# A line of 64 bytes between the weight ring and the blocks of a two-layer decoder

## The chip, the cores and the metric

The kernel runs on one core of one Trainium2 chip. The time is device microseconds of one execution, the median of several runs; lower is better. TensorE (PE in the profile, with its weight loads apart as PEld) multiplies, VectorE (DVE) and ScalarE (ACT) do elementwise work, GpSimd (POOL) fills constants, and SyncE (SP) issues most of the loads from memory.

## The reference, cut to what matters

Two layers over 256 tokens of width 2048 in fp32. Each layer has a mixer and a feed-forward part, each with a norm before it, a shift and a scale made from a vector c, a norm behind it, a gate made from c, and a residual add.

```python
for i in range(DEPTH):
    mixer, aw, ab, m_pre, m_post, f_pre, f_post, wg, wu, wd = layers[i]
    sh_m, sc_m, gt_m, sh_f, sc_f, gt_f = ada_modulation(c, aw, ab)   # silu(c) @ w + b, in 6 parts
    h = rmsnorm(x, m_pre) * (1.0 + sc_m) + sh_m
    x = x + gt_m * rmsnorm(mixer(h), m_post)
    h = rmsnorm(x, f_pre) * (1.0 + sc_f) + sh_f
    x = x + gt_f * rmsnorm(swiglu(h, wg, wu, wd), f_post)
```

The first mixer runs a diagonal state space (S5) and a gated delta rule beside each other, the second a gated linear attention; their projections and the feed-forward matrices (2048 x 5632 and back) are most of the work. The output is x, 256 x 2048.

## The kernel before

All weights stream through a ring of tiles. A tile `w` of 128 x 1024 fp32 (4,096 bytes in each partition) is loaded on SP's queue; ScalarE casts it to `wh` (line 159) and VectorE makes the remainder `wl` = w - wh (line 160). The activations are split the same way beforehand, into hi and lo halves (`hhi`/`hlo`, `ahi`/`alo` and so on). Three matmuls then give one fp32-like product: hi x hi, hi x lo, lo x hi (lines 234 to 236 in `mm3`). Of the two operands of a matmul, one (`lhsT`) is loaded into the array as weights, 128 x 128 at a time, and the other (`rhs`) streams through it.

Three routines use `mm3`. `gemm_wide` and `gemm_feat` load 128 columns of a weight tile into the array and stream 256 tokens of the activations: 256 columns a matmul. `gemm_tok` loads 128 tokens of the activations and streams 512 columns of the weight tile: 512 columns a matmul. `gemm_wide` does the gate and up projections of the feed-forward parts, `gemm_feat` the mixers' inputs (one call of it is only 16 columns wide), `gemm_tok` the rest. At the end of some products, the last weights are "held": they are cast into tiles of the block pool instead of the ring (`hwh`, `hwl`), and the matmuls of the second half of the tokens come after all those of the first half.

The order of the work is a list-scheduled program order with priorities; side streams (the shift, scale and gate vectors from `ada_w`, the S5 and delta rule parts) are advanced at fixed rates by `tick`. Nothing of this is touched by the change.

What is touched is where tiles lie in SBUF, the on-chip memory of 128 partitions. Each pool takes one stretch of bytes in every partition, one behind the other:

| pool | what it holds | first byte before | after | first byte modulo 1,024, before and after |
|---|---|---|---|---|
| cst | masks, ones, small vectors | 16,512 | 16,512 | 128, 128 |
| ring | 6 `w`, 3 `wh`, 3 `wl` of 4,096 bytes | 22,912 | 22,912 | 384, 384 |
| sm | small tiles of many sizes, the accumulator `acc` first | 72,064 | 72,064 (the new line), `acc` at 72,128 | 384, 448 (`acc`) |
| blk | 32 blocks of 4,096 bytes: x, hhi, hlo, ahi, alo, hwh, hwl, ... | 97,600 | 97,664 | 320, 384 |

Ring tiles and blocks are multiples of 4,096 bytes long, so all of a pool lie at the same place modulo 1,024. A slice of 128 columns is 512 bytes long, one of 256 columns 1,024 bytes. The operands of a ring-fed matmul thus lie 64 bytes apart (modulo 512) before.

Of the kernel before, what the change touches and what calls it, by code (L numbers as in the profile page):

```python
# [12 lines left out]
F32 = mybir.dt.float32  # L13
# [9 lines left out]
P = 128  # L23
# [4 lines left out]
LINE = 16  # L28
# [15 lines left out]
class Net:  # L44
# [49 lines left out]
    def consts(s):  # L94
        nc = s.nc

        def mask(name, op, cm, step, base=0):
            t = s.cst.tile([P, P], F32, name=name)
            nc.gpsimd.memset(t, 1.0)
            nc.gpsimd.affine_select(out=t, in_=t, pattern=[[step, P]], compare_op=op, fill=0.0, base=base, channel_multiplier=cm)  # L100
            return t

        s.ident = mask("ident", ALU.is_equal, 1, -1)
        s.uinc = mask("uinc", ALU.is_ge, -1, 1)
        s.ustr = mask("ustr", ALU.is_gt, -1, 1)
        s.lstr = mask("lstr", ALU.is_gt, 1, -1)
        s.ones = s.cst.tile([P, P], F32, name="ones")
        nc.gpsimd.memset(s.ones, 1.0)

        s.sel = s.cst.tile([P, LINE], F32, name="sel")[:, 0:1]  # L110
        nc.vector.tensor_reduce(out=s.sel, in_=s.ident[:, 0::32], axis=AX.X, op=ALU.add)
# [1502 lines left out]
```

## Time and profile before

| | us |
|---|---|
| median of 3 runs | 2570.17 |
| lowest, highest | 2564.59, 2575.0 |
| the profiled execution | 2571.89 |
| its span | 2570.1 |
| its TensorE busy | 2471.8 |
| its VectorE, ScalarE, GpSimd busy | 1731.2, 1110.6, 85.8 |
| mean granted TensorE clock | 0.981 |

The span is the time from the first to the last instruction of the profiled execution; about 2 us of the time lie around it. The first 640 us are the shift and scale of the first norm, the first mixer and its output; up to about 1400 the first feed-forward part runs, up to about 1850 the second mixer, and then the second feed-forward part. Busy times of matmuls overlap, because one starts before the one ahead has ended, so the page's mean of one matmul is longer than the distance between two starts.

### The profile page before, as it was taken

The page shows a single profiled execution, that of the slowest core. Times are in us where ns is not written, and L with a number is a line of the kernel's source. Part 1 is how long each engine was busy: PE and PEld are TensorE (multiplying, and loading weights), DVE is VectorE, ACT ScalarE, POOL GpSimd, SP SyncE. Part 2 cuts the span into 40 slices and gives each one's busy share as a digit, 9 for nine tenths or more (in the row PEclk, how much of TensorE's full clock was granted, in tenths as well). Part 3 has the DMA queues.
Part 4 walks back from the last instruction along what each step waited for, and adds up shares of the span by engine and source line. Part 5 has one row for each costly group of instructions (what it writes and reads, how often), then busy time and mean ns, then how long its engine had stood idle before and what let it go on. Part 6 is the DMA issues. An engine that isn't in the chain of part 4 may idle for free.

```text
span 2570.1 us, 41866 instructions
## 1 busy us (share of the span) xinstructions
PE 2471.8 (96%) x16822; PEld 2181.0 (85%) x16822; DVE 1731.2 (67%) x2274; ACT 1110.6 (43%) x1396; POOL 85.8 (3%) x135
## 2 busy tenths in 40 slices
PE   5999999987999999999999999999999999999998
PEld 2577989976899899988987898788799889988996
DVE  6766787689677767777778676677655444555456
ACT  3354543445434444333435633444544444443443
POOL 1120001000000000000000000000000000000000
PEclk8999999998999999999999999999999999999999
DMA  8887557577788889898886596788467666666664
GB/s 280 303 249 238 176 189 269 178 268 240 240 291 295 308 287 313 293 310 315 289 275 216 160 301 210 251 282 276 168 210 220 191 196 191 196 192 194 193 193 140
DMA packets 299012, 615.62 MB, mean 240 GB/s; under 512 B 24368, under 2 KB 61680, under 8 KB 298816
## 3 DMA queue, kind: packets, MB, share of 16 engines
q1 hardware_dynamic: 294240, 604.32, 71.4%
q0 software_dynamic: 2304, 4.93, 0.6%
q10 hardware_dynamic: 2272, 3.68, 0.4%
q8 instruction: 132, 2.16, 0.3%
q14 instruction: 64, 0.52, 0.1%
HBM read 610.10 MB, written 2.10 MB: 238 GB/s over the span
## 4 chain that ended last, share of the span: by engine, by line
PE 82%; DVE 7%; DMA 6%; ACT 3%; issue 2%; POOL 0%; ACTq 0%; DVEq 0%; SPq 0%
PE mm L236 24%; PE mm L235 24%; PE mm L234 24%; DMA w<-in_ada_w_dram 5%; PE tp L329 2%; DVE wl L160 2%; DVE small L355 1%; PE tp L365 1%; ACT small L421 1%; ACT small L462 1%; PE tp L1296 1%; PE tp L1290 1%; PE tp L1049 1%; PE tp L400 0%; DMA w<-in_w_out_dram 0%
## 5 line engine op out<-in xcount | busy, mean ns | idle before, releaser
L159 ACT CAST wh<-w 128x1024 fp32r<-128x1024 f32 x722 | 758.2, 1051 | 1100.3 <-PE mm L235 549.4
L160 DVE TENSOR_TENSOR wl<-w,wh 128x1024 fp32r<-128x1024 f32 x722 | 876.5, 1221 | 480.9 <-ACT wh L159 479.3
L236 PE MATMUL mm<-hhi,wl 128*128 128x256 f32 (+1 forms) x3104 | 866.9, 279 | 14.3 <-DVE wl L160 14.3
L234 PE MATMUL mm<-hhi,wh 128*128 128x256 f32 (+1 forms) x3104 | 867.6, 280 | 0.0
L235 PE MATMUL mm<-hlo,wh 128*128 128x256 f32 (+1 forms) x3104 | 864.9, 279 | 0.0
L236 PEld LDWEIGHTS mm<-hhi,wl 128*128 128x128 f32 (+1 forms) x3104 | 582.5, 188 | 19.0 <-DVE wl L160 17.2
L234 PEld LDWEIGHTS mm<-hhi,wh 128*128 128x128 f32 (+1 forms) x3104 | 583.3, 188 | 4.1 <-issue 1.2
L235 PEld LDWEIGHTS mm<-hlo,wh 128*128 128x128 f32 (+1 forms) x3104 | 584.0, 188 | 2.1 <-issue 1.0
L355 DVE SCALAR_TENSOR_TENSOR small<-w,silu_c,small 128x1024 f32<-128x1024 f32 x288 | 370.6, 1287 | 185.8 <-DMA w<-in_ada_w_dram 176.8
L236 PE MATMUL mm<-wh,alo 128*128 128x512 f32 x656 | 258.3, 394 | 0.0
L235 PE MATMUL mm<-wl,ahi 128*128 128x512 f32 x656 | 256.9, 392 | 0.0
L234 PE MATMUL mm<-wh,ahi 128*128 128x512 f32 x656 | 256.7, 391 | 0.0
L234 PE MATMUL mm<-wh,hhi 128*128 128x512 f32 x440 | 177.4, 407 | 6.8 <-DVE hhi L467 3.7
L235 PE MATMUL mm<-wl,hhi 128*128 128x512 f32 x440 | 177.0, 403 | 3.8 <-DVE wl L160 3.8
L236 PE MATMUL mm<-wh,hlo 128*128 128x512 f32 x440 | 175.6, 400 | 0.2 <-DVE hlo L468 0.2
L235 PEld LDWEIGHTS mm<-wl,ahi 128*128 128x128 f32 x656 | 123.2, 188 | 29.2 <-DVE wl L160 0.6
L234 PEld LDWEIGHTS mm<-wh,ahi 128*128 128x128 f32 x656 | 123.2, 188 | 27.0 <-ACT wh L159 0.5
L236 PEld LDWEIGHTS mm<-wh,alo 128*128 128x128 f32 x656 | 123.3, 188 | 25.6
L234 PEld LDWEIGHTS mm<-wh,hhi 128*128 128x128 f32 x440 | 83.8, 192 | 25.5 <-DVE hhi L467 4.4
L235 PEld LDWEIGHTS mm<-wl,hhi 128*128 128x128 f32 x440 | 84.6, 192 | 23.9 <-DVE wl L160 5.4
L236 PEld LDWEIGHTS mm<-wh,hlo 128*128 128x128 f32 x440 | 84.6, 192 | 20.1 <-DVE hlo L468 0.8
L329 PE MATMUL tp<-w,silu_c 128*32 128x512 f32 x384 | 68.9, 640 | 10.1 <-ACT silu_c L323 5.4
(432 smaller groups left out, 2433.2 us busy)
## 6 DMA issues: line engine op xcount, KB each, us to landing
w<-in_ada_w_dram SPq DMA_DIRECT2D x384, 512.0 KB, 5.2
w<-in_ffn_gate_dram SPq DMA_DIRECT2D x176, 512.0 KB, 4.5
w<-in_ffn_up_dram SPq DMA_DIRECT2D x176, 512.0 KB, 4.5
w<-in_ffn_down_dram SPq DMA_DIRECT2D x176, 512.0 KB, 4.5
w<-in_w_in_dram SPq DMA_DIRECT2D x160, 512.0 KB, 5.0
w<-in_w_out_dram SPq DMA_DIRECT2D x64, 512.0 KB, 5.4
w<-in_s_glu_w_dram SPq DMA_DIRECT2D x8, 512.0 KB, 4.8
x<-in_x_dram SPq DMA_DIRECT2D x4, 512.0 KB, 6.5
```

Of the source, the lines that this page charges most:

```text
L159: s.nc.scalar.copy(hi, x)
L160: s.subs.append(s.nc.vector.tensor_tensor(out=lo, in0=x, in1=hi, op=ALU.subtract).ins)
L234: mm(ps, lhsT=lhs[0], rhs=rhs[0], start=st, stop=False)
L235: mm(ps, lhsT=lhs[0], rhs=rhs[1], start=False, stop=False)
L236: mm(ps, lhsT=lhs[1], rhs=rhs[0], start=False, stop=en)
L329: s.nc.tensor.matmul(ps[32 * j : 32 * j + 32, :], lhsT=lhsT, rhs=w, start=first, stop=last)
L355: nc.vector.scalar_tensor_tensor(out=acc, in0=wv[:, 0], scalar=s.sc[:, g : g + 1], in1=acc, op0=ALU.mult, op1=ALU.add)
L365: s.nc.tensor.matmul(ps[:, m : m + 1], lhsT=acc[:, m * P : m * P + P], rhs=e[:, 0:1], start=True, stop=True)
L421: s.nc.scalar.activation(out=dump[:, : int(x.free_size())], in_=x, func=AF.Square, accum_out=out)
L462: nc.scalar.activation(out=hf[:, js], in_=ps[:, js], func=AF.Identity, scale=S[:, k : k + 1], bias=H[:, k : k + 1])
L1049: nc.tensor.matmul(pp[:, i * 64 : i * 64 + 64], lhsT=s.s5_win[ig][e][:, i * P : i * P + P], rhs=us[:, i * 64 : i * 64 + 64], start=True, s ...
L1290: nc.tensor.matmul(pp[:, n * 64 : n * 64 + 64], lhsT=LT[m][:, n * P : n * P + P], rhs=Tv[:, n, :, 0, :], start=True, stop=True)
```

## The change

A tile `line` of 16 floats (64 bytes in a partition) is taken from the small pool before anything else of that pool, and set to zero; nothing reads it. All small tiles and all blocks lie 64 bytes further on; the constants and the ring stay. Ring and blocks then both lie at 384 modulo 1,024.

```diff
         s.ustr = mask("ustr", ALU.is_gt, -1, 1)
         s.lstr = mask("lstr", ALU.is_gt, 1, -1)
+
+        s.line = s.sm.tile([P, LINE], F32, tag="line", name="line", bufs=1)
+        nc.gpsimd.memset(s.line, 0.0)
         s.ones = s.cst.tile([P, P], F32, name="ones")
         nc.gpsimd.memset(s.ones, 1.0)
```

On POOL, at the start of the program, the masks and constants are filled in this order before:

```order
L100 AFFINE_SELECT lstr<-lstr 128x128
L108 MEMSET ones 128x128
L1135 MEMSET lev 128x256
L1140 AFFINE_SELECT lev<-lev 128x64 x3
L1141 AFFINE_SELECT lev<-lev 128x64 x3
```

And on POOL at the same place after (all lines behind the change are numbered three higher):

```order
L100 AFFINE_SELECT lstr<-lstr 128x128
L109 MEMSET line 128x16
L111 MEMSET ones 128x128
L1138 MEMSET lev 128x256
L1143 AFFINE_SELECT lev<-lev 128x64 x3
```

The new memset stands between the mask `lstr` and `ones`. On every engine all other instructions stand in the same order as before, the 13,920 matmuls of lines 234 to 236 (237 to 239 after) included.

## The prediction

> **What bounds the kernel now.** I read the page first (busy time, chain), then the busy time by stage, then the groups of matmuls, and then the starts of single matmuls, since the change touches nothing but addresses.
>
> ```profile
> span 2570.1 us, 41866 instructions
> PE 2471.8 (96%) x16822; PEld 2181.0 (85%) x16822; DVE 1731.2 (67%) x2274; ACT 1110.6 (43%) x1396; POOL 85.8 (3%) x135
> PE 82%; DVE 7%; DMA 6%; ACT 3%; issue 2%; POOL 0%; ACTq 0%; DVEq 0%; SPq 0%
> ```
>
> TensorE is busy for 96% of the span and is 82% of the chain that ended last. A change of a few nanoseconds per matmul therefore reaches the end, unless something else is waiting just behind. By stage (columns: PE, PEld, DVE, ACT, POOL busy, granted clock, DMA share, GB/s):
>
> ```profile
> 256.00:640.00 384.00, 358.38 (x2585) 312.11 (x2584) 301.80 (x487) 177.22 (x272) 20.66 (x25) 0.94 0.66 220
> 640.00:1440.00 800.00, 780.00 (x5350) 715.54 (x5349) 583.86 (x586) 335.80 (x391) 15.83 (x23) 0.99 0.84 285
> 1440.00:1850.00 410.00, 401.20 (x2198) 340.34 (x2196) 300.55 (x433) 195.09 (x260) 8.38 (x12) 0.99 0.73 237
> 1850.00:2570.00 720.00, 710.10 (x5019) 660.85 (x5017) 370.46 (x349) 297.76 (x310) 0.35 (x1) 1.00 0.61 192
> ```
>
> From 1850 on nothing but TensorE can be the bound: DMA is 61% busy and DVE half. From 640 to 1440 DMA is 84% busy, so some of a gain there may be lost. The first 640 us hold most of the idle time and half their waits are of other engines.
>
> **The matmuls that the change concerns.** In each, one operand comes from the ring (wh, wl) and the other from a block (hhi, ahi, ...). The name before the comma streams through the array, the one after it is the weight that was loaded.
>
> ```profile
> L234 PE MATMUL mm<-hhi,wh 128*128 128x256 f32 x3072 | 858.6, 280 | 0.0
> L234 PE MATMUL mm<-wh,ahi 128*128 128x512 f32 x656 | 256.7, 391 | 0.0
> L234 PE MATMUL mm<-wh,hhi 128*128 128x512 f32 x440 | 177.4, 407 | 6.8 <-DVE hhi L467 3.7
> L234 PE MATMUL mm<-wh,yhi 128*128 128x512 f32 x104 | 41.3, 397 | 0.0
> L234 PE MATMUL mm<-wh,yahi 128*128 128x512 f32 x64 | 26.6, 416 | 1.2 <-ACT y L490 1.2
> L234 PE MATMUL mm<-wh,ybhi 128*128 128x512 f32 x48 | 19.9, 425 | 3.8 <-ACT wh L159 3.8
> ```
>
> Each row stands for three (lines 234, 235, 236), so there are 9,216 with 256 columns, and 3 x 1,312 = 3,936 with 512 columns. The durations overlap; what counts is the distance from one start to the next.
>
> **Step 1: 512 columns.** The trace holds the state after the change already. Held weights (hwh, hwl) are blocks themselves, so there both operands lie at the same place within 1,024 bytes. The ring's lie 64 bytes apart. First and last of 189 ring matmuls, then of 47 held ones:
>
> ```profile
> 2279.79 0.39 PE L234 MATMUL mm<-wh,ahi 128*128 128x512 f32 x1
> ...
> 2322.82 0.39 PE L236 MATMUL mm<-wh,alo 128*128 128x512 f32 x1
> ...
> 1384.40 0.39 PE L235 MATMUL mm<-hwl,ahi 128*128 128x512 f32 x1
> ...
> 1394.82 0.39 PE L236 MATMUL mm<-hwh,alo 128*128 128x512 f32 x1
> ```
>
> Ring: 43.03 / 188 = 0.2289 us. Held: 10.42 / 46 = 0.2265 us. The other held stretches settle at the same 0.2267, and the ring's long ones all at 0.2289. The difference is 2.2 ns, and 2.2 ns x 3,936 = 8.7 us. Summed pair by pair over the timeline, the ring's 512-column starts lie 9.5 us beyond 226.67 ns each. Some of that comes right after a wait, where held matmuls also need several to settle. I take 8 us of TensorE time as gone.
>
> **Step 2: 256 columns.** Here the timeline shows two rhythms in the same code, each kept for hundreds of matmuls. By weight loads in four stretches (columns: PEld busy and count, clock, DMA share, GB/s), three slow, the last fast:
>
> ```profile
> 1470.10:1543.20 73.10, 73.10 (x622) 1.00 0.87 280
> 1882.00:2011.50 129.50, 129.50 (x1102) 1.00 0.67 212
> 953.50:1026.60 73.10, 73.10 (x622) 1.00 0.87 297
> 2102.20:2275.60 173.40, 173.40 (x1532) 1.00 0.63 195
> ```
>
> A count includes one or two that reach in over the edge. Slow: 73.10 / 620.5 = 117.8 ns; fast: 173.4 / 1530.4 = 113.3 ns. The fast one is just half of the 226.67 ns of step 1, so I take it for the undisturbed rate. The clock is 1.00 in all four, and DMA is as busy in a slow one (0.67) as in the fast one (0.63), so neither sets the rhythm; it is chosen when a stretch starts and then stays. The three slow stretches cost 2,341 x 4.45 ns = 10.4 us. With the shorter ones and the starts after waits, the 256-column starts lie 16.0 us beyond 113.33 ns each, summed pair by pair.
>
> No 256-column pair of full width lies at distance 0 before. The nearest evidence is the 16-column projection of the second mixer, in which the weight moves on by 64 bytes with each slice of K while the block's place within 1,024 bytes stays. The matmuls of line 234, one per slice (two others between):
>
> ```profile
> 1438.04 0.28 PE L234 MATMUL mm<-hhi,wh 128*16 128x256 f32 x1
> ...
> 1438.38 0.28 PE L234 MATMUL mm<-hhi,wh 128*16 128x256 f32 x1
> ...
> 1438.74 0.28 PE L234 MATMUL mm<-hhi,wh 128*16 128x256 f32 x1
> ...
> 1439.08 0.28 PE L234 MATMUL mm<-hhi,wh 128*16 128x256 f32 x1
> ...
> 1439.42 0.28 PE L234 MATMUL mm<-hhi,wh 128*16 128x256 f32 x1
> ```
>
> Steps of 0.34, 0.36, 0.34, 0.34 us. At the first row the weight is 256 bytes on from the block (0 modulo 256); the slow step belongs to 64 and 128 bytes on. The same four-slice pattern comes back twice in this pass, and at a distance of 0 modulo 256 every matmul of it starts after 113 or 114 ns. So distance decides, with a period of 256 bytes here, and 0 is a good place. The weights are loaded 16 columns wide there, not 128, which is why this is not proof. Bounds for the 256-column matmuls: all at 113.3 gains 16.0 us; all at 117.8 instead of their mean of about 115.05 loses 2.75 ns x 9,216 = 25 us. I take the near end, less 2 us for restarts after waits (an estimate): 14 us.
>
> **Step 3: what else moves.** The small pool and the blocks move by 64 bytes together, so their distance to each other stays. Distances to the ring and the constants change for DVE and ACT too. The trace has both distances:
>
> ```profile
> L160 DVE TENSOR_TENSOR wl<-w,wh 128x1024 fp32r<-128x1024 f32 x720 | 875.7, 1224 | 480.9 <-ACT wh L159 479.3
> L160 DVE TENSOR_TENSOR hwl<-w,hwh 128x1024 fp32r<-128x1024 f32 x40 | 48.2, 1220 | 4.7 <-ACT hwh L159 4.7
> L159 ACT CAST wh<-w 128x1024 fp32r<-128x1024 f32 x720 | 757.4, 1053 | 1100.1 <-PE mm L235 549.4 <-PE mm L236 408.9 <-DMA w<-in_w_in_dram 33.0
> L159 ACT CAST hwh<-w 128x1024 fp32r<-128x1024 f32 x40 | 40.6, 1053 | 12.0 <-DMA w<-in_ffn_down_dram 7.0 <-DMA w<-in_w_out_dram 5.0
> ```
>
> Ring to ring (distance 0) against ring to block (64): 1224 and 1220 ns, 1053 and 1053. These engines cost nothing either way. The other 2,900 matmuls (16,822 on TensorE, less the 13,920 of lines 234 to 236) run in short bursts behind waits; those with a constant as operand change their distance by 64 bytes. At 4.45 ns each way they could give or take 13 us at the very most; I take 0, and 3 us for the range. The new memset of 128x16 has its like on POOL:
>
> ```profile
> L872 POOL MEMSET s5cos<- 128x16 f32 x2 | 0.2, 125 | 0.0
> PE mm L236 <- DVE wl L160: 11.4, 12, 2.1
> ```
>
> It delays the ones behind it by 0.1 us, on an engine that is 3% busy; ones is first read long after. No other instruction moves on any queue.
>
> **The sum.** Of the 22 us of TensorE time (14 + 8), by the pair-by-pair sums, 1.1 lie before 256 us, 2.1 up to 640, 7.3 up to 1440, 4.7 up to 1850 and 6.7 behind. Between 640 and 1440 TensorE waits 11.4 us for DVE's second halves (the last row above, of the waits from 640 to 1400), and DMA is at 84%; a faster TensorE asks for weights 1% sooner and will wait a little more, so I count 90% there, 95% in the next stage, all after 1850, and about half before 640. That is 0.6 + 1.3 + 6.6 + 4.5 + 6.7 = 19.7 us. The profiled execution took 2571.9 us and is 1.7 above the median of the runs shown: 2571.9 - 20 = 2552, and against the median 2550. What is late next is the cast and subtraction of a weight tile, as now.
>
> **The rivals.**
> (a) Only the 512-column matmuls gain; the 256-column ones at distance 0 keep both rhythms, taken by chance. For it: the rhythm was not a matter of distance alone before. Against it: the 16-column pass. 8.7 x 0.9 = 8 us: 2562.
> (b) Slower: at distance 0 every 256-column stretch falls into the 117.8 rhythm. Place: the 256-column stretches of both feed-forward layers. Price: +25 us, less 8 for the 512s, times 0.9: 2586. The slow share is about 39% now (1.75 of 4.45 ns); from 58% the loss eats the 8 us of the 512s, and from 94% the kernel is slower by 0.5%. Against it: half of 226.67 is 113.33, and the loads of a 512-column matmul meet its stream in the same way.
> (c) Weight loads and streaming do not disturb each other at all, and both rhythms have another cause: 2570. The spread of the three runs, 10 us, would then be all there is. The Trainium skill, SBUF — State Buffer, section "Who interferes with whom", says so: it gives the matmul's stream and the weight load independent read ports and lets TensorE wait for nobody. By that rule step 1's two spacings would be one; the trace has 228.9 and 226.5 for the same shape with DMA at work in both, so I follow the trace.
> (d) The gain is taken back by supply: DMA or DVE waits grow by as much from 640 to 1850. Then only what lies behind 1850 and a little more stays, some 9 us: 2561. Against it: only 11.4 us of waiting there now.
>
> **Numbers.** Forecast 0.70, (a) 0.12, (b) 0.08, (c) 0.06, (d) 0.04. About 0.5% (13 us) can be told from no change. The forecast's own range is 2541 to 2557: all 25.5 us and 3 for the other matmuls at the low end, 13 us of gain at the high end. To leave out no more than 2 in 10 the range goes on through (a) and (d) to 2566. Faster: nearly all of the forecast, 0.68. Same: (a), (c), (d) and a little of the forecast, 0.24. Slower: (b), 0.08.
>
> **What would show it.** Right: ring-fed 512-column starts 226.7 ns apart in long stretches, 256-column starts at 113.3 in every long stretch, TensorE's waits for DVE up by a few us at most. Step 1 is wrong if 228.9 stays; step 2 if stretches at 117.8 are still there; the sum if both are gone and the span is not about 20 us shorter. What would make me wrong most easily is step 2, where the width of the load differs from the only evidence.

## The result: the kernel became slower by 1%

The changed kernel takes 2597.71 us (median of 5 runs, 2595.65 to 2599.52), against 2573.6 us for the kernel before, run beside it (5 runs, 2564.59 to 2579.66). The ratio over the runs is 1.0104, with an interval of 1.0086 to 1.0122 (the two medians alone give 1.0094). The prediction was 2550 us, faster. The profiled execution took 2597.71 us too.

Page of the kernel after, the lines of the span, the busy times and the chain:

```profile
span 2596.0 us, 41867 instructions
PE 2500.4 (96%) x16822; PEld 2218.5 (85%) x16822; DVE 1731.9 (67%) x2274; ACT 1108.5 (43%) x1396; POOL 85.3 (3%) x136
PE 78%; DMA 8%; DVE 8%; issue 3%; ACT 3%; POOL 0%; DVEq 0%; ACTq 0%; SPq 0%; POOLq 0%
```

Only TensorE moved: its busy time grew by 28.6 us (2471.8 to 2500.4) and that of its weight loads by 37.5, while the other engines are within 2.1 us of before. The span grew by 25.9 us.

Busy time by stage of the kernel after (columns: PE, PEld, DVE, ACT, POOL busy, granted clock, DMA share, GB/s):

```profile
256.00:640.00 384.00, 358.39 (x2591) 313.02 (x2590) 304.71 (x490) 176.08 (x272) 20.64 (x25) 0.96 0.66 220
640.00:1440.00 800.00, 784.69 (x5295) 723.70 (x5295) 581.09 (x581) 334.56 (x390) 15.81 (x23) 1.00 0.84 282
1440.00:1860.00 420.00, 409.39 (x2241) 348.47 (x2240) 300.42 (x434) 195.54 (x261) 8.72 (x12) 0.99 0.73 235
1860.00:2596.00 736.00, 726.02 (x5011) 679.49 (x5009) 370.96 (x349) 296.65 (x310) 0.00 (x0) 1.00 0.63 187
```

From 640 to 1440 us, where the first feed-forward part runs, TensorE was busy longer (784.7 against 780.0) and got through fewer matmuls (5,295 against 5,350). The clock and the DMA share are those of before, so neither explains it. The last stage, again mostly a feed-forward part, now takes 736 us instead of 720.

Groups of matmuls and of DVE's subtraction, after (line, engine, operation, operands and shapes, count, busy us, mean ns of one, idle time before them):

```profile
L237 PE MATMUL mm<-hhi,wh 128*128 128x256 f32 x3072 | 873.7, 284 | 0.0
L237 PE MATMUL mm<-wh,ahi 128*128 128x512 f32 x656 | 256.3, 391 | 0.0
...
L163 DVE TENSOR_TENSOR wl<-w,wh 128x1024 fp32r<-128x1024 f32 x720 | 875.9, 1224 | 503.9 <-ACT wh L162 502.9
```

The 256-column matmul grew from 280 to 284 ns; the 512-column one stayed at 391. DVE's subtraction takes 1224 ns as before. These means overlap, so the distances from start to start decide. The 256-column ones first, by weight loads in three long stretches after (columns: PEld busy and count, clock, DMA share, GB/s):

```profile
963.00:1030.00 67.00, 66.29 (x554) 1.00 0.90 304
1900.00:2030.00 130.00, 128.65 (x1054) 1.00 0.71 212
2118.00:2290.00 172.00, 172.00 (x1435) 1.00 0.63 184
```

The last row is the plainest: 172.00 us for 1,435 loads, less the one or two that reach in over the edge, is 120.0 ns each. Single matmuls inside it say the same (first and last of 185), and beside them stand the first and the last of 191 ring-fed 512-column ones:

```profile
2119.81 0.28 PE L239 MATMUL mm<-hhi,wl 128*128 128x256 f32 x1
...
2141.89 0.28 PE L237 MATMUL mm<-hhi,wh 128*128 128x256 f32 x1
...
2299.81 0.39 PE L239 MATMUL mm<-wh,alo 128*128 128x512 f32 x1
...
2342.88 0.39 PE L237 MATMUL mm<-wh,ahi 128*128 128x512 f32 x1
```

256 columns: 22.08 / 184 = 0.1200 us. 512 columns: 43.07 / 190 = 0.2267 us. All 15 long stretches of 256 columns (94 to 1,535 matmuls) run at 120.0 ns; neither 113.3 nor 117.8 occurs any more. The time that starts lie beyond 113.33 and 226.67 ns each, summed pair by pair over the timeline as in the prediction, gives the account. Gaps of about 1.3 times these distances and more are left out of the first two rows; what they are over stands in the row of the long gaps:

| | before, us | after, us | difference |
|---|---|---|---|
| 256 columns, beyond 113.33 ns | 16.05 | 61.55 | +45.5 |
| ring-fed 512 columns, beyond 226.67 ns | 9.5 | 1.8 | -7.7 |
| all other matmuls (transposes and the like), all their time | 351.2 | 346.8 | -4.4 |
| long gaps after ring-fed and held matmuls | 95.6 | 88.4 | -7.2 |
| sum | | | +26.2 (the span: +25.9) |

The profile's own idle time of TensorE fell less, from 98.3 to 95.6 us, since its modelled ends cover the short gaps. A slower TensorE gives DVE more time, and the waits for DVE's second halves bear that out. First those of before, then of after (us in total, times, longest):

```profile
PE mm L236 <- DVE wl L160: 14.3, 14, 2.4
PE mm L235 <- DVE wl L160: 5.0, 6, 1.5
```

```profile
PE mm L239 <- DVE wl L163: 5.9, 7, 2.4
PE mm L238 <- DVE wl L163: 8.5, 11, 2.1
```

Lines 235 and 236 are lines 238 and 239 after: together these waits fell from 19.3 to 14.4 us. The profiles of experiments 2, 3 (four lines), 4 and the control of 7, whose distances are those of before, have 16.6 to 22.8 us of them; those with two and three lines, slower still, have 12.0 and 15.3.

### The profile page after: what moved, and what is told of

It is laid out like the page before. It is cut to its first block, busy times and chain, and to the rows that moved or that the text cites. A ratio compares the mean times of both kernels' runs of the same rounds, so it can differ in the third digit from the quotient of the medians.

```text
span 2596.0 us, 41867 instructions
## 1 busy us (share of the span) xinstructions
PE 2500.4 (96%) x16822; PEld 2218.5 (85%) x16822; DVE 1731.9 (67%) x2274; ACT 1108.5 (43%) x1396; POOL 85.3 (3%) x136
## 4 chain that ended last, share of the span: by engine, by line
PE 78%; DMA 8%; DVE 8%; issue 3%; ACT 3%; POOL 0%; DVEq 0%; ACTq 0%; SPq 0%; POOLq 0%
PE mm L238 23%; PE mm L239 23%; PE mm L237 23%; DMA w<-in_ada_w_dram 6%; DVE wl L163 2%; DVE small L358 2%; PE tp L332 1%; PE tp L368 1%; ACT small L424 1%; ACT small L465 1%; DMA small<-in_ada_b_dram 1%; PE tp L1299 1%; PE tp L1293 1%; PE tp L1052 1%; DMA w<-in_w_in_dram 0%
## 5 line engine op out<-in xcount | busy, mean ns | idle before, releaser
L239 PE MATMUL mm<-hhi,wl 128*128 128x256 f32 (+1 forms) x3104 | 881.0, 284 | 6.0 <-DVE wl L163 5.9
L237 PE MATMUL mm<-hhi,wh 128*128 128x256 f32 (+1 forms) x3104 | 882.9, 284 | 0.0
L238 PE MATMUL mm<-hlo,wh 128*128 128x256 f32 (+1 forms) x3104 | 880.0, 284 | 0.0
L239 PEld LDWEIGHTS mm<-hhi,wl 128*128 128x128 f32 (+1 forms) x3104 | 593.9, 191 | 9.4 <-DVE wl L163 7.7
L237 PEld LDWEIGHTS mm<-hhi,wh 128*128 128x128 f32 (+1 forms) x3104 | 594.1, 191 | 4.1 <-issue 1.2
L238 PEld LDWEIGHTS mm<-hlo,wh 128*128 128x128 f32 (+1 forms) x3104 | 593.9, 191 | 2.1 <-issue 1.0
L237 PEld LDWEIGHTS mm<-wh,hhi 128*128 128x128 f32 x440 | 83.7, 192 | 25.2 <-DVE hhi L470 4.8
```

Of the source, the lines that this page charges most:

```text
L237: mm(ps, lhsT=lhs[0], rhs=rhs[0], start=st, stop=False)
L238: mm(ps, lhsT=lhs[0], rhs=rhs[1], start=False, stop=False)
L239: mm(ps, lhsT=lhs[1], rhs=rhs[0], start=False, stop=en)
```

## The experiments

In all that follows, the distance is the first byte of the operand that streams, minus the first byte of the weights that are loaded, modulo 256 where that is enough. Before, it was 192 for the 256-column matmuls (the blocks stream) and 64 for the ring-fed 512-column ones (the ring streams); after, it is 0 for both.

The question was what decides 120.0. The first theory: each matmul loses a time that the distance alone sets, with a period of 256 bytes, whatever its number of columns. The second, that of the prediction: the undisturbed rate is 17/16 of the streaming time (113.3 and 226.7 ns), nothing is ever faster, and 256 columns pay extra at distance 0 for another reason. Later a third thing had to be settled: what picks 113.3 or 117.8 at one and the same distance.

**1. A map of the distance, nothing else running (m1_map).** The computation is left out; stretches of 45 matmuls alternate between two halves as `mm3` does, and only the place of the stream moves.

```python
a = A[1 if j == 2 else 0][:, (k % 8) * 128 : (k % 8) * 128 + cols]   # weights
b = B[1 if j == 1 else 0][:, off : off + N]                          # stream, `off` floats on
nc.tensor.matmul(ps[:cols, :N], lhsT=a, rhs=b, ...)
```

> A kernel that leaves the whole computation out: it writes zeros and runs stretches of 45 matmuls, with weights from one pair of tiles and the stream from another, the stream 0 to 960 bytes on from the weights in steps of 64 (twice), in steps of 16 below 256, at 256 and 512 columns, some at 192 and 384 columns, and some with 16 instead of 128 weight columns. Theory 1: TensorE streams a column every 0.417 ns, and each weight load adds a fixed price that depends on the distance (place of the stream less place of the weights) modulo 256 and not on the number of columns. From the two traces the price is 13.3 ns at 0 (226.7 - 213.3 and 120.0 - 106.7), 15.6 at +64 (228.9 - 213.3) and 6.7 or 11.1 at -64 (113.3 or 117.8 - 106.7). So at distance 0: 192 columns 93.3 ns, 384 columns 173.3, 256 columns 120.0, 512 columns 226.7; at +64: 256 columns 122.3; at -64 (192): 512 columns 220.0 or 224.4; and every 256 bytes the same again. Theory 2 (the prediction's): the undisturbed rate is 17/16 of 0.417 ns a column, nothing is ever faster than 113.3 or 226.7, and 256 columns pay extra at distance 0 for another reason: 384 columns at 0 take 170 or more with an extra, 512 columns at -64 at least 226.7.

Timeline of this kernel, one row for a stretch (start, us from its first start to its last end, operands, count). The first ten rows are distances 0, 64, 128, 192 and 256, each with 256 and then 512 columns; then 960 with 256 columns, 0 with 384 columns, and 16-column loads at 0 and 192:

```profile
39.42 5.64 PE L26 MATMUL ps<-B,A 128*128 128x256 f32 x45 [0.68 <-ACT o L27]
45.59 10.49 PE L26 MATMUL ps<-B,A 128*128 128x512 f32 x45 [0.52 <-ACT o L27]
56.81 5.57 PE L26 MATMUL ps<-B,A 128*128 128x256 f32 x45 [0.73 <-ACT o L27]
62.90 10.59 PE L26 MATMUL ps<-B,A 128*128 128x512 f32 x45 [0.52 <-ACT o L27]
74.22 5.60 PE L26 MATMUL ps<-B,A 128*128 128x256 f32 x45 [0.73 <-ACT o L27]
80.34 10.73 PE L26 MATMUL ps<-B,A 128*128 128x512 f32 x45 [0.52 <-ACT o L27]
91.80 5.57 PE L26 MATMUL ps<-B,A 128*128 128x256 f32 x45 [0.73 <-ACT o L27]
97.88 10.76 PE L26 MATMUL ps<-B,A 128*128 128x512 f32 x45 [0.52 <-ACT o L27]
109.37 5.65 PE L26 MATMUL ps<-B,A 128*128 128x256 f32 x45 [0.73 <-ACT o L27]
115.54 10.49 PE L26 MATMUL ps<-B,A 128*128 128x512 f32 x45 [0.52 <-ACT o L27]
...
301.95 5.39 PE L26 MATMUL ps<-B,A 128*128 128x256 f32 x45 [0.73 <-ACT o L27]
...
815.93 8.08 PE L26 MATMUL ps<-B,A 128*128 128x384 f32 x45 [0.46 <-ACT o L27]
...
868.32 5.28 PE L26 MATMUL ps<-B,A 128*16 128x256 f32 x45 [0.62 <-ACT o L27]
...
885.71 5.47 PE L26 MATMUL ps<-B,A 128*16 128x256 f32 x45 [0.51 <-ACT o L27]
```

A stretch starts irregularly and its length holds the last matmul's own end, so the settled distance between starts was taken from the 16th start on, in ns:

| distance | 256 columns | 512 columns | 384 columns | 256 columns, 16-column loads |
|---|---|---|---|---|
| 0 | 120.0 | 226.7 | 173.3 | 113.3 |
| 64 | 117.8 | 229.0 | 173.3 | 113.3 |
| 128 | 118.6 | 232.4 | 176.0 | 113.3 |
| 192 | 117.8, once 113.3 (the 301.95 row) | 233.2 | 173.3 | 117.8 |

Distances 256, 512 and 768 repeat the row of 0 (the rows at 109.37 and 115.54 against the first two), so the period is 256 bytes. 192 columns take 111.6 ns at every distance. Of the other multiples of 16 bytes, 112 gave 113.3 with 256 columns and the rest 117.3 to 119.9; with 512 columns they gave 231.2 to 236.6.

The map gives the spacings of the result. It has 120.0 and 226.7 at distance 0, as the kernel after does; 229.0 and the two rhythms 113.3 and 117.8 at the distances of before; and it has them with no DMA, DVE or ACT at work. At distance 0 the three sizes lie on one line: from 256 to 512 columns the distance grows by 106.7 ns, 0.4167 ns a column, and 120.0 - 106.7 = 173.3 - 160.0 = 226.7 - 213.3 = 13.3 ns remain, the streaming time of 32 columns. So the first theory holds at 0, where it had named 173.3 for 384 columns; an extra that were a share of the streaming time would not stay at 13.3 ns for three sizes. Away from 0 the first theory fails: the extra of 128 is 11.9 ns with 256 columns and 19.1 with 512, and at 192 the 512 columns take 233.2 ns where it wanted 220.0 or 224.4. The bounds that the second theory had named (no less than 113.3 and 226.7, and 170 or more for 384 columns) are broken by no row here, but it had no price for distance 0. The price has to be read from a map, column count by column count.

**2. The line behind everything (e1_line_behind).** The tile and its memset stay, but in a pool that comes after the blocks, so no other tile moves.

```diff
+        s.end = ent(name="end", bufs=1)        # opened after the blocks
-        s.line = s.sm.tile([P, LINE], F32, tag="line", name="line", bufs=1)
+        s.line = s.end.tile([P, LINE], F32, tag="line", name="line", bufs=1)
```

> The line and its memset stay, but the line lies behind the blocks, so that no other tile moves. Theory 1 (the distance of ring and blocks): as before, 2573.6 us, within 0.3%; 256-column starts again in two rhythms (113.3 and 117.8 ns), ring-fed 512-column starts at 228.9. Rival (the added instruction or its effect on the start of the program): as after, 1.0% slower, about 2598.

2575.47 against 2574.63 us, ratio 1.000 (0.9983 to 1.0017). Both rhythms and 228.9 are back; the sums beyond 113.33 and 226.67 ns are 16.4 and 10.5 us. The memset and the tile cost nothing; the place does it all.

**3. Two, three and four lines (e2, e3, e4).** `LINE` becomes `2 * LINE`, `3 * LINE`, `4 * LINE` in the same statement:

```diff
-        s.line = s.sm.tile([P, LINE], F32, tag="line", name="line", bufs=1)
+        s.line = s.sm.tile([P, 2 * LINE], F32, tag="line", name="line", bufs=1)
```

> Two lines instead of one: blocks and small tiles lie 128 bytes further on than before, blocks 64 bytes on from the ring. Theory 1, with a price per load that depends on the distance alone: 256-column starts at 106.7 + 15.6 = 122.3 ns (the 512-column price of before), +7.2 ns x 9,327 = +67 us of TensorE time against before; ring-fed 512-column starts at 220.0 to 224.4, -34 to -18 us; together +33 to +49 us, of which some 0.7 reach the end as after: 2597 to 2608. Theory 2: 256 columns at 113.3 or more, 512 columns at 226.7 or more; 2565 to 2600.

> Three lines: blocks lie 128 bytes on from the ring, so the distance is 128 modulo 256 for both shapes. No trace so far shows 128-column loads at this distance. Theory 1 says only that the time follows from what the map of distances shows at 128: price x 9,327 and x 3,736 against before's means of 8.4 ns (115.05 - 106.67) and 15.9 ns (229.2 - 213.3), times 0.7. If 128 costs as 0 does, 2598; if a load costs nothing there, 2573.6 - 0.7 x (78 + 59) = 2478. Rival (places modulo 1,024 count, or only the same place): about 2570, as before or better than after by 26 us.

> Four lines: blocks lie 256 bytes further on than before, so the distance is the one of before modulo 256 and another one modulo 512 and 1,024. Theory 1 with the period of 256 bytes that the map shows: as before, ratio 1.000 within 0.3%, 512-column starts at 228.9 and 256-column starts in the two rhythms 113.3 and 117.8. Rival (the place within 1,024 bytes, the change's own words): a time of its own, off by about 1% as with one, two and three lines.

| lines | distance, 256 and 512 columns | us | ratio | beyond 113.33 and 226.67 ns, us |
|---|---|---|---|---|
| 0 (before) | 192, 64 | 2573.6 to 2574.95, beside the rows below | 1 | 16.05, 9.5 |
| 1 (after) | 0, 0 | 2597.71 | 1.0104 (1.0086 to 1.0122) | 61.55, 1.8 |
| 2 | 64, 192 | 2602.6 | 1.0107 (1.0087 to 1.0127) | 40.6, 25.2 |
| 3 | 128, 128 | 2611.34 | 1.0141 (1.0119 to 1.0163) | 52.7, 22.4 |
| 4 | 192, 64 | 2571.73 | 0.9989 (0.997 to 1.0008) | 12.8, 9.5 |

Groups of the kernel with two lines:

```profile
L237 PE MATMUL mm<-hhi,wh 128*128 128x256 f32 x3072 | 861.8, 281 | 0.0
L237 PE MATMUL mm<-wh,ahi 128*128 128x512 f32 x656 | 260.0, 396 | 0.0
```

Here the 512-column group rose from 391 to 396 ns, while the 256-column one is only 1 ns above before: with two lines the loss sits in the other family of matmuls. Its starts settle at 233.3 ns, and the 256-column ones at 117.8 in all long stretches but two, both as on the map for 192 and 64. The first theory had wanted 122.3 and 220 to 224 there; the total came out in its range only because the two errors cancel. The second theory's 2565 to 2600 was missed by 3 us. With three lines the map's 118.6 and 232.4 would give about 2605 us by the formula of the expectation, against 2611.34. Part of the difference is that distance 128 has two rhythms as well in the kernel, 118.7 and 120.0 ns with 256 columns (1,536 matmuls in one stretch at 120.0) and 232.4 and 233.3 with 512, where the map of experiment 1 had shown the lower one of each alone. Four lines are 256 bytes, a full period, and bring the time of before back, although the distance modulo 512 and modulo 1,024 is another one there. Of the four distances that whole lines can set, that of before is the best.

**4. The line ahead of the ring (e5_line_before_ring).** Ring, small tiles and blocks all move by 64 bytes together, against address zero and against the four masks that are taken before the line (the identity matrix of the transposes among them). The constants taken after it move along.

```diff
-        s.line = s.sm.tile([P, LINE], F32, tag="line", name="line", bufs=1)
+        s.line = s.cst.tile([P, LINE], F32, name="line")
```

> The line lies in front of the ring, so that ring, small tiles and blocks all lie 64 bytes further on: the blocks are where the changed kernel has them, but ring and blocks are 64 bytes apart as before. Theory 1 (distance of ring and blocks): as before, ratio 1.000 within 0.3%. Rival (the absolute place of the blocks, or their distance to the constants, which is that of the changed kernel): 1.01, about 2600.

2574.51 against 2574.95 us, ratio 0.9998 (0.9981 to 1.0015), with 19.6 and 10.9 us beyond. A shift of 64 bytes in the absolute place and in the distance to the masks costs nothing; the distance between ring and blocks is what counts.

**5. The two halves at different distances (m2_two_distances).** Again without the computation. In `mm3` one operand has a hi and a lo half in the ring; here the low half lies f bytes further on than the high one.

```python
PLAN.append((256, (0, f), (e, e), 45, 1 + r))   # weights at 0 and f, streams at e (in floats)
PLAN.append((512, (e, e), (0, f), 45, 1 + r))   # the other way round
PLAN.append((256, (0, 0), (48, 48), 45 + r % 3, 1 + r % 4))   # 12 times: distance 192, starts varied
```

> Again a kernel that leaves the whole computation out and runs stretches of 45 matmuls. Now the ring's second halves (wl) may lie elsewhere than the first (wh): blocks e bytes on from wh, wl f bytes on from wh, e and f 0, 64, 128, 192, each pair three times at 256 columns (weights from the ring) and at 512 (weights from the blocks); then the distance of before (e 192, f 0) twelve times more at 256 columns, after pauses of one to four copies. Theory 1 (each weight load has a price set by its distance, modulo 256, to the stream it runs beside): with f 0 the first map again (256 columns 120.0, 117.8, 118.6, 117.8 or 113.3 ns; 512 columns 226.7, 233.2, 232.4, 229.0 at e 0, 64, 128, 192); with f above 0 values between these; a pair with 256 columns at 113.3 every time and 512 columns under 229.0 would make a faster kernel. Of the twelve, some at 113.3 and some at 117.8, if the rhythm is a matter of how a stretch starts; all alike, if it is a matter of places alone.

With f = 0 the map came back, but for one 113.3 at distance 64 and two 233.2 with 512 columns at 128. The pair at 192 with the low half 128 on gave 113.3 ns in both stretches at the full clock (a third had a lower granted clock and is left out), with 512 columns at 230.3 to 230.6. The twelve stretches at 192 alone take turns. Timeline, four of them:

```profile
942.26 5.57 PE L26 MATMUL ps<-B,A 128*128 128x256 f32 x45 [1.96 <-ACT o L28]
...
961.88 5.38 PE L26 MATMUL ps<-B,A 128*128 128x256 f32 x45 [1.32 <-ACT o L28]
...
981.73 5.57 PE L26 MATMUL ps<-B,A 128*128 128x256 f32 x45 [0.92 <-ACT o L28]
...
1002.16 5.39 PE L26 MATMUL ps<-B,A 128*128 128x256 f32 x45 [0.52 <-ACT o L28]
```

Equal matmuls, equal places, equal counts: 5.57 us (117.8 ns) and 5.38 (113.3). At 192 two rhythms are stable, and something in how a stretch starts, or in what ran before it, picks one. The pauses take turns too: after one or three copies between two of these stretches comes 113.3, after two or four 117.8. Experiment 6 shows that the length of the pause alone is not it: there both rhythms follow on pauses of one and of two copies, and 117.8 on those of three.

**6. Twelve starts for each distance (m3_starts).** No computation; 256 columns only.

```python
for r in range(12):
    for i in range(len(PLACES)):   # all places in a mixed order; counts of 45 to 48
        ...
        PLAN.append((256, (0, f), (e, e), 45 + (SEED >> 12) % 4, 1 + (SEED >> 20) % 3))
```

> A kernel that leaves the whole computation out: 256-column matmuls alone, in stretches of 45 to 48, at 16 distances (0 to 240 bytes in steps of 16, wl as far as wh) and 12 more with wl at a place of its own, each started 12 times after different pauses and in a mixed order. Theory 1a (distance sets which rhythms are possible, the start picks one): 0 at 120.0 every time; 192 at 113.3 in about half the starts and at 117.8 in the others, as in the kernel before (some 60 to 40); 64 mostly 117.8. A distance with 113.3 at every start would be worth 16 us of TensorE time. Theory 1b (distance alone): each distance has one value.

| distance (low half further on) | settled ns over 12 starts |
|---|---|
| 0 | 120.0 (12) |
| 64 | 117.8 (11), 113.3 (1) |
| 96 | 120.0 (12) |
| 112 | 113.3 (12) |
| 128 | 118.7 (12) |
| 192 | 117.8 (8), 113.3 (4) |
| 192 (+128) | 113.3 (12) |
| 64 (+128) | 118.9 (7), 113.3 (5) |

These are eight of the 28 places that ran. So distance 0 is bad from all twelve starts, 192 is a matter of the start, and 192 with the halves 128 apart is good from all twelve. The starts differ in the pause and in the number of matmuls, hardly in what ran before: the stretch ahead of 192, for instance, was the one at 16 bytes eleven times out of twelve.

**7. Give each family its best distance (e6_two_places) and a control (e7_two_places_control).** `wh` and `wl` become slices of three larger tiles, so `gemm_wide` and `gemm_feat` can keep the distance of before (192) while `gemm_tok` gets 0. The control has the same tiles with the distances of before for all three.

```diff
+        t = s.ring.tile([P, (2112, 2112, 2064)[i]], F32R, tag=f"wc{i}", name="wc", bufs=1)
+        return t[:, at : at + 1024], t[:, at + 1024 : at + 2048]
...
-                wh = s.ring.tile([P, 1024], F32R, tag="wh", name="wh", bufs=s.WH)
-                wl = s.ring.tile([P, 1024], F32R, tag="wl", name="wl", bufs=s.WH)
+                wh, wl = s.pair(at)    # at=16 floats for gemm_wide and gemm_feat;
+                                       # for gemm_tok 0 (e6) or 16 (e7)
```

> Each distance where it pays: wh and wl lie together in one of three larger tiles; gemm_wide and gemm_feat (256 columns) use it from 64 bytes on, gemm_tok (512 columns) from its start, and the blocks lie at the same place as that start. So 512-column matmuls have distance 0 and 256-column matmuls that of before. Since wh and wl come free together, some 250 rows of the program order differ a little from before. Theory 1: ring-fed 512-column starts at 226.7 and 256-column starts in the two rhythms of before: 7.7 us of TensorE time less than before, some 6 of it at the end: 0.9977 of before. Rival (both shapes are bound to one state that the blocks' place sets): 256 columns at 120, 1.01 of before.

> The same tiles and the same program order as the kernel with two places, but gemm_tok too uses the tiles from 64 bytes on, so that all distances are those of before. Theory 1: 512-column starts at 228.9 again, and the time 6 us (0.23%) above the kernel with two places; against before only the joint release of wh and wl shows, within 0.3%.

e6: 2586.62 against 2575.41 us, ratio 1.0037 (1.002 to 1.0054). e7: 2577.02, ratio 1.0005 (0.9993 to 1.0017). Groups, first two of e6, then one of e7 (`wc` is the tile of both halves):

```profile
L241 PE MATMUL mm<-hhi,wc 128*128 128x256 f32 x3072 | 866.2, 282 | 0.0
L241 PE MATMUL mm<-wc,ahi 128*128 128x512 f32 x656 | 256.5, 391 | 0.0
```

```profile
L241 PE MATMUL mm<-hhi,wc 128*128 128x256 f32 x3072 | 858.7, 280 | 0.0
```

The 512-column starts went to 226.7 ns in e6 (2.1 us beyond instead of 10.6 in the control), as meant. But the 256-column ones, whose places are the same in both kernels, fell mostly into the slow rhythm: 32.3 us beyond, 16.1 in the control, where all of them at 117.8 would be 41. A change to `gemm_tok` alone thus made other matmuls slower. The control says that it isn't the tiles. It is hardly chance either: in before, in experiments 2 and 4, with four lines and in the control the three longest stretches came out alike (1,103 matmuls at 117.8 ns, 1,536 and 1,152 at 113.3), and in e6 all three are at 117.8. It fits experiment 5: how a stretch starts, or what ran before it, sets its rhythm. What exactly does it was not found.

**8. The pair that is good from every start (e8_halves_apart).** A gap of 128 bytes between the `wh` and the `wl` tiles of the ring, and the line made 128 bytes: distance 192 for 256 columns, with the low half 128 further on.

```diff
-        s.line = s.sm.tile([P, LINE], F32, tag="line", name="line", bufs=1)
+        s.line = s.sm.tile([P, 2 * LINE], F32, tag="line", name="line", bufs=1)
...
                 wh = s.ring.tile([P, 1024], F32R, tag="wh", name="wh", bufs=s.WH)
+                if s.gap is None:
+                    s.gap = s.ring.tile([P, 2 * LINE], F32, tag="gap", name="gap", bufs=1)
+                    s.nc.gpsimd.memset(s.gap, 0.0)
                 wl = s.ring.tile([P, 1024], F32R, tag="wl", name="wl", bufs=s.WH)
```

> wl lies 128 bytes further on against wh (a gap in the ring), the blocks as far from wh as before modulo 256 (two more lines in the small pool). In the map of starts this pair of distances, 192 and 128, is one of two with 113.3 ns at all twelve starts; the earlier map has 512 columns there at 230.3 to 230.6. Theory 1a (the distances set the possible rhythms): every long 256-column stretch at 113.3, -16 us of TensorE time; 512-column starts at about 230.4, +5 us; together -11, some 8 at the end: 0.997 of before. Rival (the kernel's starts, which hold more than such stretches, find the slow rhythm all the same): 256 columns partly at 117.8, 1.00 or above.

2569.13 against 2575.8 us, ratio 0.9975 (0.9962 to 0.9987): the only kernel here that beats the one before. Weight loads of a stretch, and the groups:

```profile
2096.00:2268.00 172.00, 172.00 (x1518) 1.00 0.63 193
```

```profile
L240 PE MATMUL mm<-hhi,wh 128*128 128x256 f32 x3072 | 854.4, 278 | 0.0
L240 PE MATMUL mm<-wh,ahi 128*128 128x512 f32 x656 | 259.0, 395 | 0.0
```

172.00 us for 1,518 loads is 113.3 ns, and every long stretch of 256 columns has it now: 2.6 us beyond, against 16.05 before. The 512-column ones pay at about 230.5 ns, 14.2 us beyond instead of 9.5. Net -8.8 us of TensorE time, and 6.7 us of the median.

**9. The distance 112 (e9_112_and_0).** The tiles of e6, with 112 for the 256-column matmuls (113.3 from all 12 starts in experiment 6) and 0 for the 512-column ones.

```diff
-            ws = s.wload(..., at=16)          # gemm_wide, gemm_feat in e6
+            ws = s.wload(..., at=4)           # gemm_tok now at=32
```

> The tiles of the kernel with two places (wh and wl in one of three larger tiles, same program order), but gemm_wide and gemm_feat use them so that the blocks lie 112 bytes on from wh and wl, the other distance at which all twelve starts had 113.3 ns; gemm_tok at distance 0. To make room, the shift and scale of the first norm share two tiles with a late one. Theory 1a: 256-column starts at 113.3 in all long stretches, 512-column starts at 226.7: -24 us of TensorE time against before, of which 0.7 to 0.85 reach the end: 0.992 to 0.994 of before. Rival (as with two places before, a 512-column part at distance 0 leaves the next 256-column part in the slow rhythm): 1.00 to 1.004.

2602.35 against 2575.8 us, ratio 1.0094 (1.0081 to 1.0108). Weight loads of a stretch, and the group:

```profile
2117.00:2290.00 173.00, 173.00 (x1443) 1.00 0.60 183
```

```profile
L241 PE MATMUL mm<-hhi,wc 128*128 128x256 f32 x3072 | 877.6, 286 | 0.0
```

173.00 / 1,441.5 = 120.0 ns, and so in all long stretches but one of 95 matmuls; the 512-column starts are at 226.7 as meant. The transfer from the map failed. One difference is in the places: in the map the weights began at a multiple of 64 bytes and the stream 48 bytes past one; here the weights begin 16 bytes past one and the stream on it. Another is what runs before a stretch: bare stretches of the same shape there, 512-column matmuls at distance 0 here. The places would mean that the distance alone does not decide where they are not multiples of 64 bytes. No run isolates either.

## Why the prediction was wrong

- What bounds the kernel: right. TensorE's net change (+33.4 us over the first three rows of the account) came through to the span as 25.9 us; shorter gaps gave 7.2 back. The waits for DVE's second halves, which the prediction had expected to grow under a faster TensorE, fell from 19.3 to 14.4 us under the slower one.
- **Step 1, 512 columns: right.** 228.9 became 226.7 ns in all long stretches; 7.7 us went, 8 were taken.
- **Step 2, 256 columns: this is the step that failed.** It took all stretches at 113.3 ns and a gain of 14 us; they run at 120.0 and lose 45.5 us. Two arguments in it broke. The first was the 16-column projection as evidence. What it says of 16-column loads is right: the map has 113.3 at 0 with them. With 128-column loads the same place gives 120.0. The width of the load, which the prediction itself named as its weakest point, is all that differs between these two rows of the map. The second was "just half of the 226.67 ns of step 1, so I take it for the undisturbed rate". The match says nothing: 226.7 is 213.3 + 13.3 with the full loss of distance 0 in it, and 113.3 is 106.7 + 6.7, the time of 16 columns. Halving a time that has a fixed part says nothing about a shape of half the length, and the same 13.3 put on 106.7 would have given 120.0.
- The bounds of step 2 failed too. The far end, 117.8 ns for all, was the slowest rhythm seen before. No 128-wide pair at distance 0 was in the trace, so nothing bounded it from above; with 120.0 the loss was 45.5 us where 25 was the most that any rival knew of.
- Step 3: right. The subtraction stays at 1224 ns, the memset costs nothing (e1), 64 bytes against the masks nothing (e5), and the other matmuls moved by 4.4 us, a little more than the 3 that the range allowed but no more than between profiles of kernels with the distances of before.
- The sum has a slip that decides nothing: half of the 2.1 us between 256 and 640 us is 1.05, not 1.3.
- Rival (b) had the sign and the place, and named the 256-column stretches as what would do it. Its price was too small, since it put them at 117.8: 2586 instead of 2597.71.
- Rival (c), by the Trainium skill's SBUF — State Buffer, "Who interferes with whom", falls. The same 512-column matmul takes 226.7, 229.0, 232.4 or 233.2 ns by distance alone, with no other engine at work. So the time of a matmul does depend on where its stream lies against its weight load, which independent ports alone do not account for.
- Rivals (a) and (d) fall with step 2: the 256-column matmuls did not stay, and TensorE's idle time did not grow.

Open are what at the start of a stretch, or before it, picks one of the two rhythms at distance 192, why distance 0 is the bad place for 128-column loads with 256 columns and the good one with 512, and why 112 did not transfer.

## What to carry to other kernels

Where matmuls each come with a load of weights of their own, the distance between the streamed and the loaded operand modulo 256 bytes can matter: here it cost 1.4% at the worst place tried and gained 0.25% at the best, and the best distance differed with the number of columns. An alignment that looks tidy can be a bad one. Map it with a bare stretch of the very shapes (load width, columns, hi and lo halves), from several starts, at the very places that the kernel will use, before moving a pool, and then run the kernel: the map of 112 bytes did not transfer. Evidence from a shape with another load width, or a rate found by halving another one, is not evidence.

## What the runs showed of the hardware that was not expected

- At distance 0 a matmul with a load of 128 columns takes its columns at 0.4167 ns each and 13.3 ns more, from 256 to 512 columns; 192 columns take 111.6 ns at every distance, more than the 93.3 of that line, so something other than streaming bounds them (the load is the likely one; not isolated).
- The loss depends on the distance with a period of 256 bytes, and differently by size: at 64 bytes 117.8 ns is below distance 0's 120.0 with 256 columns, while 229.0 is above 226.7 with 512.
- At distance 192 two rhythms, 113.3 and 117.8 ns, are each stable for a whole stretch, and a change to matmuls that run earlier, of another shape and at another place, can change which one is taken (e6 against e7: 16 us of TensorE time with not one address of the slower matmuls changed).
